# Other step durations and a minimum stay in the planner that merges TensorE's streams

## The chip, the core and the metric

One core of a Trainium2 chip runs the whole program. The time is the device time of one execution in microseconds (us); of several executions the median is given. Five engines work side by side, each through its own list of instructions in order: TensorE (PE, with its weight loads, PEld), VectorE (DVE), ScalarE (ACT), GpSimd (POOL) and SyncE (SP), which here issues the transfers.

## The reference, cut to what matters

One inference step of a decoder of two layers, for a prompt of 1024 tokens and 8 samples of one token each, all float32. Width 1024, heads of 64:

```python
def hybrid_layer(x, pos, x_prev, wkv0, kv_buf, v_first, lp):
    p = x @ w_comb                                    # q|k|v of 8 heads, r|k|v and low-rank inputs of 8 more
    q, k = rope(q, pos), rope(k, pos)
    att = dilated_attention(q, k, v)                  # three bands (128,1), (512,4), (2048,16), merged
    att = att * rsqrt(mean(att ** 2) + eps) * gain
    z = token_shift(pr, prev0, shift_mu)
    rw, v_first, S_T = rwkv7_time_mix(z, v_first, wkv0, lp)    # delta-rule state, step by step in time
    mix = concat([att, rw]) @ w_out
    x1 = layer_norm(alpha * x + mix)
    y = layer_norm(alpha * x1 + relu(x1 @ w_ff_up) ** 2 @ w_ff_down)
```

The samples do the same with a state of their own (the state update of the mixer, called decode in the kernel) and with attention over 1024 cached keys (called kv).

## The kernel before

The tokens lie along the free axis, in two halves of 512 (the second with the 8 samples behind it). Every **dense** product (in-projection, out-projection, the two products of the feed-forward part) is made of output tiles of 128 channels by 256 to 512 tokens. Operands are split into a high and a low part, so that one step over 128 inputs is three matmuls (L364, L365, L366, into a PSUM tile dps). Weights come from HBM (wr), are split by ACT (L337, wh) and DVE (L338, wl) and wait in a ring of four pieces.

Beside it run **small groups** of PE work: a few matmuls or transposes each, whose result another engine reads before the next group of the same stream can go on.

- *Stage 1* of the mixer (function stage1; groups psg, pn, pl, pt1, pt2, pbn) takes 256 tokens of a pair of heads, a unit, up to the inverses of its triangular blocks. For the second half's last unit it ends in pdv, which hands the samples' inputs to decode.
- *Stage 2* (stage2; pT1, pBV, pX, pPQ, pO, pz, pgm, pgv) is a serial chain: inverses, outputs, and from pO to pz and back the state over four blocks of 64 tokens. There are 4 pairs of 2 units in each half of each layer.
- *Attention* (attention; pS, pET, pFT, po, pof), a pair of heads at a time. Its operands are fetched by att_load (L1494: transfers stg<-d_qkv) and split by casts on ACT (L1515, L1519) and subtractions on POOL.
- *decode* (L1639 and on): from pdv through DRAM, then in four passes a load of the samples' states (ST, L1648), products on DVE and POOL and a store (L1657), then through DRAM again (d_y, then dyr, L1666) to the groups pdy, pdm and pdq.
- *post* and *kv*: projected values to time-major, and the samples' attention over their caches (pds, pdo).

What sets PE's order is the class **Streams**. Each stream is a Python generator. A step emits one group with all that follows from it on other engines, and yields what the group costs in ns, which PSUM tag it holds and for how long, and when the next group's operands will be there. Streams.run keeps a clock of its own, self.now, that only these numbers move. At each turn it goes through the streams in the order of their adding (s2, s1, att, post, kv, and dense as the last) and takes the first that is ready by its clock, else the one that will be ready first. So small groups go ahead whenever their latency, times a slack of 1.2 in the first half-layer and 2.2 later (SLK), has passed, and the dense stream fills what is left. One brake is there: where the dense stream is ready, a small stream that has done more of its phase than the dense stream has of the phase beside it (times PACE, plus LEAD; method ahead, with the table WORK of what each phase costs) is passed over. PE follows the order that comes out word for word; for the other engines the framework makes the order.

The dense stream waits for the small ones at few places, among them those where the mixer's and the attention's outputs are needed (Mix.wait: s2, at, and for the second half dec and kv): for the last half-layer this is near the end of the feed-forward part of layer 1, first half, just ahead of the groups lnc of its second LayerNorm. After it, there is nothing but dense work and LayerNorm.

```python
                if t <= self.now:                      # Streams.run, the turn's choice
                    best = (t, s)
                    break
...
                cost += 3 * (n / 2.4 + 2.5)            # dense_steps, a step's cost for n tokens
...
            yield from mixes[l, 1].wait()              # half, ahead of the last LayerNorm of layer 1, first half
```

Of the kernel before, what the change touches and what calls it, by code (L numbers as in the profile page):

```python
# [16 lines left out]
PSUM = bass.MemoryType.PSUM  # L17
# [28 lines left out]
        "dense": (519e3, 536e3, 382e3, 394e3)}  # L46
# [76 lines left out]
def _rope():  # L123
    """Cosines and signed sines of each half's positions, and of the samples' position."""
# [14 lines left out]
def bc(ap, dims):  # L139
    """View of a tile with free dims given as (stride, count) pairs."""  # L140
    return bass.AP(tensor=ap.tensor, offset=ap.offset, ap=[list(ap.ap[0])] + [list(d) for d in dims])


class Streams:
    """Merges the emission of several instruction streams so that the TensorE's program order keeps it busy.

    A stream is a generator. Each step emits one group for the TensorE (and what follows from it on the other
    engines) and yields (cost, (bank, hold), latency, next bank): the time the group takes, the PSUM tag that it
    holds and for how long, when the next group's operands are there, and the tag that the next group needs.
    A stream may also yield a function: it goes on when that returns a time."""  # L150

    def __init__(self, depth):
        self.now = 0.0
        self.depth = depth
        self.hist = {b: [] for b in depth}
        self.streams = []
        self.times = {}
        self.cost = {}
        self.phase = {}
        self.work = {}  # L160

# [15 lines left out]
    def share(self, name):  # L177
        """The part of a stream's phase that is done."""
# [3 lines left out]
    def ahead(self, s):  # L182
        """Whether a stream has done more of its phase than the last stream of the phase beside it."""
# [35 lines left out]
    def run(self):  # L219
        while self.streams:  # L220
            best = None
            main = self.ready(self.streams[-1])
            for s in self.streams:
# [3 lines left out]
                if main is not None and main <= self.now and s is not self.streams[-1] and self.ahead(s):  # L227
                    continue
# [7 lines left out]
            self.step(best[1])  # L236


def bc(ap, dims):
    """View of a tile with free dims given as (stride, count) pairs."""  # L240
# [4 lines left out]
def body(ctx, tc, I, O):  # L245
# [44 lines left out]
    def xc(t, k, c, m=1):  # L290
        """Columns of x: tile k, or the m tiles from there."""
# [20 lines left out]
    class Weights:  # L312
        """Streams weight tiles in order of use, in pieces of four K tiles split into two float32r parts."""
# [28 lines left out]
        def take(self, keep=False):  # L342
            """The next tile's pieces; those that are kept stay in the ring until release()."""
# [11 lines left out]
    def dense_steps(items, kts, xhh, xll, res):  # L355
        """Output tiles of a dense product, side by side, in steps; their PSUM tiles are appended to res."""
        pts = [bank("d", "dps") for _ in items]
        last = len(kts) - 1
        for i, (wk, kt) in enumerate(kts):
            cost = 0  # L360
            for p, (w, m, c0, n) in zip(pts, items):
# [5 lines left out]
                cost += 3 * (n / 2.4 + 2.5)  # L367
# [5 lines left out]
    def dense(items, kts, xhh, xll, evac):  # L373
        """Dense tiles with their evacuations; a generator of steps."""
        res = []
# [27 lines left out]
    def proj_specs(l, h):  # L403
        """Weight tiles of an in-projection in order of use; the first ones come once per chunk after a LayerNorm."""
# [9 lines left out]
    def rest_specs(l, h):  # L414
        wo, wu, wd = I["w_out"], I["w_ff_up"], I["w_ff_down"]

        def inx(o):
            """Where in x, while it is free, a tile's weights stay for both chunks."""
# [6 lines left out]
        def aside(o):  # L425
            """The same where the next half's operands already lie in the first tiles of x."""
# [62 lines left out]
    def state_load(l, col, n):  # L489
        """The samples' shift states as columns of x."""  # L490
# [23 lines left out]
    def shifted(l, h, mus, m, idx, put):  # L514
        """Evacuation of an in-projection tile with the token shift; put(ci, c0, n, tile) stores a chunk."""
# [25 lines left out]
    def sigmoid(e):  # L541
        """1 / (1 + e) in place, for e = exp(-x)."""
# [3 lines left out]
    def in_proj(l, h, hook=None, tail=None, then=None):  # L546
        """The in-projection of a half: the low-rank inputs, then r, k, v (shifted) and q, k, v of each pair. hook
        comes after each of the first tiles of the first chunk, tail after the first pair's r, k, v, then before the last
        q, k, v."""
# [101 lines left out]
    def rope(t, n, tabs):  # L651
        """Rotates a pair's queries or keys: the first halves of its heads in partitions 0 to 63, the second below."""
# [7 lines left out]
    def post_stream():  # L660
        """Projected values to time-major; the samples' queries, keys and values to rows."""
# [29 lines left out]
    class LayerNorm:  # L691
        """LayerNorm over the channels of src into t, chunk by chunk of the tokens; src's tiles arrive one at a
        time. The sums are taken about the mean of the first tile. If bare, t lacks the offset in the end."""
# [49 lines left out]
        def scale(self, m, behind=None):  # L743
            """The next m tiles of a chunk whose sums are there."""
# [21 lines left out]
    class Mix:  # L766
        """The out-projection's operands of a half: the mixer's rows split, the attention's rows normalised."""
# [70 lines left out]
    def half(l, h, prev=None):  # L838
        """The dense part of a layer for one half of the tokens, and the next layer's in-projection. prev is what
        the half before left to be done beside the first tiles."""  # L840
# [33 lines left out]
        def passes(tile, ln):  # L874
            """Tiles o over all chunks, chunk by chunk, with LayerNorm's sums; a chunk's end comes beside the next
            one's tiles."""
# [146 lines left out]
        elif h == 0:  # L1023
            def beside(o):
                """The half's end beside the next one's first tiles."""
# [11 lines left out]
    def init():  # L1037
        """Constants that the start doesn't need."""
# [38 lines left out]
    def stage1(l, h, p, u, s, lw, out):  # L1077
        """Everything of a unit up to the inverses of its triangular blocks."""
# [772 lines left out]
```

## Time and profile before

| | us |
|---|---|
| median of 3 runs | 3624.27 (3622.15 to 3625.78) |
| span of the profiled execution | 3630.6 |
| PE busy in it | 3287.2 (91%) |
| DVE busy | 2060.3 (57%) |
| ACT busy | 1449.6 (40%) |
| POOL busy | 972.0 (27%) |

The profiled execution took 6.3 us more than the median of the runs; a sum made on its span is brought to the runs by that. PE's busy time is made of spans that overlap: a matmul's span goes on while the next one has started, so what a matmul costs is read from the distance between starts in the timeline. [...]

### The profile page before, as it was taken

The numbers are of one execution on the slowest core, as the hardware profiler recorded it, in microseconds if no ns is written. First come the engines' busy times: TensorE is split into PE (matmuls) and PEld (weight loads), VectorE is DVE, ScalarE is ACT, GpSimd is POOL, SyncE is SP. The second block draws the span as 40 slices with busy tenths as digits, with TensorE's granted clock in tenths as the row PEclk, the third lists the DMA queues.
The fourth block names the chain that finished last, engine by engine and source line by source line (L and its number), as shares of the span: only waits on it lengthen the run. The fifth ranks groups of instructions, "written<-read, shape, count | busy, mean of one in ns | idle before, by whom it ended". The sixth has DMA issues, their size and how long they took to land.

```text
span 3630.6 us, 66265 instructions
## 1 busy us (share of the span) xinstructions
PE 3287.2 (91%) x24732; PEld 2747.8 (76%) x24732; DVE 2060.3 (57%) x4703; ACT 1449.6 (40%) x3266; POOL 972.0 (27%) x1841
## 2 busy tenths in 40 slices
PE   8797997979899998888999999798898999989998
PEld 6565776766677677677889998676675777789998
DVE  4454544665555665467655557456654564685556
ACT  4344433343343244344443335334343433453334
POOL 1323232541111322335211013334412121240012
PEclk9898998989899999998999999898898999999999
DMA  6333343524333335442333335444143333333332
GB/s 218 106 107 108 110 120 93 141 77 116 109 108 86 101 92 155 142 136 80 85 97 88 85 88 153 117 125 132 53 119 104 109 111 89 116 99 92 94 89 84
DMA packets 366249, 393.45 MB, mean 108 GB/s; under 512 B 141816, under 2 KB 218824, under 8 KB 365928
## 3 DMA queue, kind: packets, MB, share of 16 engines
q1 hardware_dynamic: 365928, 389.22, 37.4%
q8 instruction: 195, 3.19, 0.4%
q14 instruction: 126, 1.03, 0.1%
HBM read 325.16 MB, written 63.97 MB: 107 GB/s over the span
## 4 chain that ended last, share of the span: by engine, by line
PE 42%; DMA 6%; DVE 5%; ACT 2%; issue 2%; SPq 1%; POOL 1%; ACTq 0%; DVEq 0%; POOLq 0%
PE dps L364 12%; PE dps L365 11%; PE dps L366 11%; DMA stg<-d_qkv 3%; DVE t L750 1%; PE pl L1180 1%; PE pX L1274 1%; DVE wl L338 1%; PE po L1603 1%; PE pO L1350 1%; PE pS L1558 1%; DVE t L731 0%; PE pS L1546 0%; PE pO L1331 0%; PE pO L1336 0%
## 5 line engine op out<-in xcount | busy, mean ns | idle before, releaser
L364 PE MATMUL dps<-xh,wh 128*128 128x256 f32 (+3 forms) x2984 | 1015.0, 340 | 29.8 <-ACT wh L337 13.0
L365 PE MATMUL dps<-xl,wh 128*128 128x256 f32 (+3 forms) x2984 | 959.0, 321 | 8.8 <-DVE xl L753 7.0
L366 PE MATMUL dps<-xh,wl 128*128 128x256 f32 (+3 forms) x2984 | 955.2, 320 | 2.6 <-DVE wl L338 2.6
L338 DVE TENSOR_TENSOR wl<-wr,wh 128x512 fp32r<-128x512 f32 (+1 forms) x772 | 572.6, 743 | 484.1 <-ACT wh L337 462.2
L337 ACT CAST wh<-wr 128x512 fp32r<-128x512 f32 (+1 forms) x772 | 474.8, 616 | 882.9 <-PE dps L365 807.0
L364 PEld LDWEIGHTS dps<-xh,wh 128*128 128x128 f32 x2984 | 578.7, 194 | 116.1 <-issue 40.7
L365 PEld LDWEIGHTS dps<-xl,wh 128*128 128x128 f32 x2984 | 579.4, 194 | 43.1 <-DVE xl L753 10.6
L366 PEld LDWEIGHTS dps<-xh,wl 128*128 128x128 f32 x2984 | 577.7, 194 | 42.8 <-DVE wl L338 4.6
L364 PE MATMUL dps<-hh,wh 128*128 128x512 f32 (+2 forms) x1600 | 542.0, 339 | 10.6 <-DVE t L894 5.1
L365 PE MATMUL dps<-hl,wh 128*128 128x512 f32 (+2 forms) x1600 | 514.1, 321 | 3.7 <-DVE hl L936 2.3
L366 PE MATMUL dps<-hh,wl 128*128 128x512 f32 (+2 forms) x1600 | 513.4, 321 | 0.0
L364 PEld LDWEIGHTS dps<-hh,wh 128*128 128x128 f32 x1600 | 305.1, 191 | 52.8 <-issue 17.3
L366 PEld LDWEIGHTS dps<-hh,wl 128*128 128x128 f32 x1600 | 305.3, 191 | 22.5
L365 PEld LDWEIGHTS dps<-hl,wh 128*128 128x128 f32 x1600 | 305.8, 191 | 21.7 <-DVE hl L936 3.0
L1203 POOL TENSOR_TENSOR tm<-BL,XB 32x15 f32<-32x15 f32 (+7 forms) x480 | 147.1, 306 | 578.6 <-DMA BL<-d_el 521.5
L967 DVE TENSOR_TENSOR t<-dps,t 128x256 f32<-128x256 f32 (+1 forms) x240 | 123.7, 516 | 170.8 <-PE dps L366 170.1
L1205 POOL TENSOR_TENSOR XB<-XB,tm 32x15 f32<-32x15 f32 (+7 forms) x480 | 156.2, 325 | 33.8
L720 POOL TENSOR_TENSOR ln<-ln,lsq 128x256 f32<-128x256 f32 (+1 forms) x112 | 91.8, 819 | 251.2 <-ACT lsq L718 247.4
L935 DVE CAST hh<-rl 128x256 fp32r<-128x256 f32 (+2 forms) x200 | 73.5, 368 | 117.2 <-ACT rl L934 114.7
L933 ACT ACTIVATE rl<-dps 128x256 f32<-128x256 f32 (+2 forms) x200 | 88.6, 443 | 107.9 <-PE dps L366 106.2
L364 PE MATMUL dps<-hh,xh 128*128 128x256 f32 (+1 forms) x368 | 115.1, 313 | 13.1 <-DVE t L1000 6.0
L709 POOL TENSOR_TENSOR t<-t,ln 128x256 f32<-128x256 f32 (+1 forms) x32 | 28.1, 915 | 366.7 <-ACT ln L703 366.7
(346 smaller groups left out, 5192.4 us busy)
## 6 DMA issues: line engine op xcount, KB each, us to landing
wr<-in_w_ff_up SPq DMA_DIRECT2D x272, 256.0 KB
wr<-in_w_ff_down SPq DMA_DIRECT2D x256, 256.0 KB
wr<-in_w_in SPq DMA_DIRECT2D x220, 256.0 KB
stg<-d_qkv SPq DMA_DIRECT2D x128, 128.0 KB
wr<-in_w_out SPq DMA_DIRECT2D x64, 256.0 KB
z<-d_z SPq DMA_DIRECT2D x24, 384.0 KB
d_qkv<-qe SPq DMA_DIRECT2D x32, 256.0 KB
kvc<-in_cache_k SPq DMA_DIRECT2D x32, 256.0 KB
```

The source lines that it names most:

```text
L337: A.copy(h[:, :, :m], w[:, :, :m])
L338: V.tensor_tensor(lo[:, :, :m], w[:, :, :m], h.bitcast(F32)[:, :, :m], op=ALU.subtract)
L364: PE.matmul(p[:m, :n], wh[:, wk % 4, :m], hi, start=(i == 0), stop=False)
L365: PE.matmul(p[:m, :n], wh[:, wk % 4, :m], lo, start=False, stop=False)
L366: PE.matmul(p[:m, :n], wl[:, wk % 4, :m], hi, start=False, stop=(i == last))
L720: G.tensor_tensor(s2, s2, sq, op=ALU.add)
L750: V.scalar_tensor_tensor(t, t, g, self.s2[:, c], op0=ALU.mult, op1=ALU.mult)
L933: A.activation(r, p[:, :n], AF.Relu)
L935: V.tensor_copy(hh[:, c0:c0 + n], r)
L967: V.tensor_tensor(to, p[:, :n], to, op=ALU.add)
L1203: G.tensor_tensor(tv, bc(BL[:, 17 * j + 1:17 * j + 2], [(1, m), (0, j + 1)]), bc(XB[:, 16 * j:16 * j + 1], [(0, m), (1, j + 1)]), op=ALU.mult)
L1205: G.tensor_tensor(xv, xv, tv, op=ALU.add)
```

## The change

The planner's numbers and its rule of choice change; what is computed and the instructions stay.

- A dense step of n tokens costs 3 x (0.447 n + 4) ns in the planner, 699 in place of 648 for 512 tokens, and the dense phases in WORK are scaled by the same 8%.
- When the planner comes back from small groups to the dense stream, its clock moves on by SWITCH = 280 ns.
- From then on it stays with the dense stream for RUN = 3200 ns of its clock, as long as this stream is ready, whatever else is. This holds once the first half-layer's dense part has been entered ("dense" in self.phase); ahead of that there is no stay.

The docstrings of the file are emptied too.

```diff
@@ constants
 WORK = {"s2": (73e3, 74e3, 73e3, 74e3), "s1": (38e3, 42e3, 42e3, 45e3), "att": (29e3, 49e3, 29e3, 49e3),
-        "dense": (519e3, 536e3, 382e3, 394e3)}
+        "dense": (561e3, 580e3, 413e3, 427e3)}
+RUN = 3200
+SWITCH = 280
@@ Streams.__init__
         self.work = {}
+        self.stay = 0.0
+        self.away = False
@@ Streams.run
         while self.streams:
             best = None
-            main = self.ready(self.streams[-1])
+            last = self.streams[-1]
+            main = self.ready(last)
+            free = main is not None and main <= self.now
+            if free and self.now < self.stay:
+                self.step(last)
+                continue
             for s in self.streams:
                 t = self.ready(s)
                 if t is None:
                     continue
-                if main is not None and main <= self.now and s is not self.streams[-1] and self.ahead(s):
+                if free and s is not last and self.ahead(s):
                     continue
...
             self.now = max(self.now, best[0])
-            self.step(best[1])
+            if best[1] is not last:
+                at = self.now
+                self.step(best[1])
+                self.away |= self.now > at
+                continue
+            if self.away:
+                self.away = False
+                self.now += SWITCH
+                if "dense" in self.phase:
+                    self.stay = self.now + RUN
+            self.step(last)
@@ dense_steps
-                cost += 3 * (n / 2.4 + 2.5)
+                cost += 3 * (0.447 * n + 4)
```

The order of PE's instructions changes nearly everywhere behind the first groups. Two places show how.

PE, attention and stage 1 beside the feed-forward part of layer 0, first half, about a quarter into the program, before; pO0 and pz are of stage 2, pt1 and pt2 of stage 1:

```order
L1350 MATMUL pO0_10034<-FG_10006,Zp_129 64x128 x2
L364 MATMUL dps_10135<-hh_8821,wh_9925 128x512
L365 MATMUL dps_10135<-hl_8822,wh_9925 128x512
L366 MATMUL dps_10135<-hh_8821,wl_9926 128x512
L1222 MATMUL pt1_10139<-cst_79,BK_9810 128x128 x4
L364 MATMUL dps_10135<-hh_9454,wh_9925 128x512
L365 MATMUL dps_10135<-hl_9455,wh_9925 128x512
L366 MATMUL dps_10135<-hh_9454,wl_9926 128x512
L1235 MATMUL pt2_10150<-cst_79,AR_9809 128x128 x4
L1357 MATMUL pz_10156<-cst_79,St_10127 64x64 x2
```

The same groups now:

```order
L384 MATMUL dps_9708<-xh0_88,wh_9581 128x512
L385 MATMUL dps_9708<-xl0_90,wh_9581 128x512
L386 MATMUL dps_9708<-xh0_88,wl_9582 128x512
L1377 MATMUL pz_9715<-cst_79,St_9613 64x64 x2
L1242 MATMUL pt1_9720<-cst_79,BK_9415 128x128 x4
L1255 MATMUL pt2_9728<-cst_79,AR_9414 128x128 x4
```

Before, one dense step of three matmuls stood between pO0, pt1 and pt2. Now pz, pt1 and pt2 follow each other, and 15 dense matmuls stand ahead of them and 15 behind, of which three are shown.

PE, where decode ends in layer 1 (pdy, pdm, pdq; the last of the mixer's groups are pgm and pgv), before:

```order
L364 MATMUL dps<-xh_88,wh 128x512
L365 MATMUL dps<-xl_90,wh 128x512
L366 MATMUL dps<-xh_88,wl 128x512
L1387 MATMUL pgv<-gq,cst 128x256
L1674 MATMUL pdm<-a,cst 128x32
```

The same place now:

```order
L1398 MATMUL pgm<-y,cst 128x256
L1399 MATMUL pgm<-gs,gup 128x256
L1407 MATMUL pgv<-gq,cst 128x256
L1690 MATMUL pdy<-cst,dyr 128x8 x4
L1694 MATMUL pdm<-a,cst 128x32
L1699 MATMUL pdq<-a,cst 128x32
L722 MATMUL lnc<-t,onec 128x256 x2
L384 MATMUL dps<-xh_88,wh 128x512
L385 MATMUL dps<-xl_90,wh 128x512
L386 MATMUL dps<-xh_88,wl 128x512
```

Before, pdy stood six dense matmuls ahead of the first row shown and pdq eighteen behind the last, and the groups lnc come some 34 us of dense work later. Now pgm, pgv and the groups of decode follow each other without a dense matmul, and lnc, at which the dense stream waits for the small ones, comes right behind.

## Rows read from the trace of the kernel before

**Rows 1.** The page, part 1: busy us of each engine, share of the span, instructions.
```profile
PE 3287.2 (91%) x24732; PEld 2747.8 (76%) x24732; DVE 2060.3 (57%) x4703; ACT 1449.6 (40%) x3266; POOL 972.0 (27%) x1841
```

**Rows 2.** Stages: stretch, us; busy us of PE, PEld, DVE, ACT, POOL; PEclk; DMA, GB/s.
```profile
51.30:678.80 627.50, 536.64 (x4266) 430.15 (x4264) 308.19 (x845) 244.71 (x589) 205.74 (x444) 0.91 0.40 115
678.80:1359.20 680.40, 622.94 (x4368) 473.43 (x4367) 391.63 (x897) 261.80 (x591) 178.22 (x355) 0.96 0.35 98
...
1430.10:2066.30 636.20, 584.30 (x4757) 501.72 (x4756) 371.58 (x873) 260.56 (x604) 187.43 (x373) 0.95 0.36 101
...
2362.10:3073.50 711.40, 647.81 (x4754) 496.26 (x4752) 412.26 (x954) 267.29 (x618) 186.95 (x371) 0.93 0.37 106
```

**Rows 3.** PE's waits of two stages, longest row each: us, times, longest.
```profile
PE pn L1139 <- ACT sg L544: 14.7, 1, 14.7
...
PE pq L679 <- issue: 12.2, 1, 12.2
```

**Rows 4.** Timeline, 735 to 756 us: start, us, engine, line; idle before and its releaser.
```profile
745.56 0.62 ACT L1519 CAST kS<-stg 128x512 fp32r<-128x512 f32 x1 [12.03 <-DMA stg<-d_qkv]
...
753.53 1.23 PE L1139 MATMUL pn<-cst,sg 128*128 128x128 f32 x4 [14.67 <-ACT sg L544]
```

**Rows 5.** ACT's waits, whole span.
```profile
ACT kS L1519 <- DMA stg<-d_qkv: 198.9, 34, 16.6
```

**Rows 6.** Stretch behind the stall of rows 4, columns as in rows 2.
```profile
753.50:757.30 3.80, 3.77 (x24) 2.96 (x25) 3.48 (x6) 2.37 (x7) 3.44 (x5) 0.50 0.13 22
```

**Rows 7.** Timeline of PE: pz alone, pl alone, pz and pl, pbn alone.
```profile
873.13 0.39 PE L365 MATMUL dps<-hl,wh 128*128 128x512 f32 x1
873.36 0.39 PE L366 MATMUL dps<-hh,wl 128*128 128x512 f32 x1
873.68 0.33 PE L1357 MATMUL pz<-cst,St 64*64 64x64 f32 x4
...
874.28 0.40 PE L365 MATMUL dps<-hl,wh 128*128 128x512 f32 x1
...
1432.87 0.39 PE L366 MATMUL dps<-xh,wl 128*128 128x512 f32 x1
1433.19 1.71 PE L1180 MATMUL pl<-AR,BK 64*128 64x128 f32 x16
...
1435.17 0.40 PE L365 MATMUL dps<-xl,wh 128*128 128x512 f32 x1
...
861.96 0.39 PE L366 MATMUL dps<-hh,wl 128*128 128x512 f32 x1
862.28 0.33 PE L1357 MATMUL pz<-cst,St 64*64 64x64 f32 x4
862.54 1.71 PE L1180 MATMUL pl<-AR,BK 64*128 64x128 f32 x16
...
864.52 0.39 PE L365 MATMUL dps<-hl,wh 128*128 128x512 f32 x1
...
1991.65 0.28 PE L365 MATMUL dps<-hl,wh 128*128 128x256 f32 x1
1991.78 0.28 PE L366 MATMUL dps<-hh,wl 128*128 128x256 f32 x1
1991.89 0.59 PE L1239 MATMUL pbn<-sq,cst 128*128 128x256 f32 x2
...
1992.44 0.28 PE L365 MATMUL dps<-hl,wh 128*128 128x256 f32 x1
```

**Rows 8.** Timeline of PE and SP: decode's input, last transfer, first group behind.
```profile
2932.09 0.27 PE L1249 MATMUL pdv<-cst,dvt 128*40 128x128 f32 x1
...
2995.53 0.30 SPq L1666 DMA_DIRECT2D dyr<-d_y  x1
...
3030.82 0.41 PE L1670 MATMUL pdy<-cst,dyr 8*128 8x8 f32 x4
```

**Rows 9.** A stretch of the second stage with few small groups, columns as in rows 2.
```profile
998.70:1278.80 280.10, 273.32 (x1826) 204.00 (x1825) 153.27 (x319) 100.05 (x210) 61.73 (x139) 0.99 0.35 98
```

## The prediction

> **What bounds the kernel now.** I read the page first, then a table of stages, then the waits of TensorE (PE) stage by stage, then single places in the timeline. On the page [rows 1] PE is busy 91% of the span and no other engine above 57%, so the kernel is one long PE program, whose order is fixed beforehand. In it stand 14904 matmuls of the dense products and 1298 small groups of the mixer and the attention, in 764 interruptions of the dense work (counted in the order). The loss is what stands between PE's busy time and the span, 343 us, and the table of stages [rows 2] says where: 90.9 us in the first stage with small groups (51 to 679 us), and 57.5, 51.9 and 63.6 us in the three later ones (679 to 1359, 1430 to 2066, 2362 to 3074), 173 us together. The other 80 us lie in four stretches with few small groups, which the change hardly touches.
>
> Who ends these waits: PE waits rarely, 29, 21 and 25 times in the three later stages, and the longest alone takes 14.7 us in the second stage and 12.2 in the last [rows 3]; 18 of the 75 are over 3 us and hold 120 of the 173 us. What is behind the longest is seen at 738 to 754 us [rows 4]: ScalarE (ACT), which works in order, stands 12.0 us at a cast until its transfer stg<-d_qkv lands, the sigmoid behind it is late, and PE stops 14.7 us at group pn. In sum ACT waits 198.9 us at these casts [rows 5]; PE covers of a stall what dense work it has ahead of the first group that needs ACT. [...]
>
> **The change part by part.** No instruction is added or removed; the docstrings that go cost nothing. PE's order changes, and with a moved group move its evacuations on VectorE and ACT and its transfers, past the weight loads in SyncE's queue; I give that no term of its own, and the ends of the later stages' term stand for it.
>
> *Fewer interruptions.* The order has 584 instead of 764. What one costs is read where PE waits for nothing [rows 7]. From the last dense matmul to the second one behind: 0.92 us around pz alone, 2.30 around pl alone, 2.56 around pz and pl together; two dense steps (0.466) are in each, so the groups cost 0.45, 1.83 and 2.09, and joining them saves 0.19. That is the switch: pz starts 0.32 us behind the last dense matmul where dense ones follow each other at 0.23, and the dense work is late again behind it. The group pbn, which uses the whole array as the dense matmuls do, starts 0.11 behind the last one, near their own spacing of 0.13: it has no switch, and joining it to pz leaves pz's where it was. A saving comes only where two groups follow each other that both use part of the array (64 rows or columns). Such neighbours number 223 before and 260 after: 37 x 0.19 = 7 us. Taken: **-7 us**; ends 0 and -36 (all 180 at 0.2).
>
> [...]
>
> *Later stages: a minimum stay.* Behind each interruption now stand at least 3.2 us of dense work, 15 matmuls at 0.233 us or 27 at 0.12 us [rows 7]. Dense runs of at most 12 matmuls fall from 379 to 16 in all stages but the first. I took each group and its successor in the same stream (pO and pz, pS and pET, and so on) and priced the PE work between them by such rows: its median goes from 3.66, 3.61 and 3.70 us in the three later stages to 4.36, 4.13 and 4.61, its tenth percentile from 2.2 to 3.5. So a successor comes some 0.9 us later, and each wait shrinks by up to that. The 18 waits above 3 us lose 16 us; the 57 short ones (53 us, mean 0.9) lose about half, 26. Together 42 us of idle time. For the clock: 0.96, 0.95 and 0.93 in these stages [rows 2] mean half speed in 8, 10 and 14% of them, 218 us for 173 us of idle time; PE is busy in part of it and loses half of that, so I take 0.4 us more for each idle us. 42 x 1.4: **-59 us**. Ends: 0, if the stalls at stg decide alone (the casts stand as close in ACT's new order as before), and -105 (all short waits, 1.2 us of each long one, x 1.4).
>
> *First stage.* There the minimum stay isn't on yet, but dense steps cost 8% more in the planner and a return 280 ns, so small groups come earlier against the dense work: 364 instead of 333 in the same dense stretch, with 1.89 instead of 2.18 us between successors (tenth percentile 1.10 for 1.38). 25 waits longer by 0.3 us, x 1.4: **+11 us**; ends 0 and +25 (a fifth of the stage's waits).
>
> *The end of the mixer.* Because they yield to the stay, the small streams of the last stage end later: the last chain step of the mixer stood 38 us of dense work ahead of the point where the dense stream waits for the streams (the lnc groups), and now the last 26 groups ahead of pdy stand at that point with no dense matmul among them, then pdy, pdm and pdq. What decides is the samples' state update (decode): from pdv, its last input, it goes through a transfer, four passes of load, VectorE, GpSimd and store, and two more transfers before pdy can run. The rows [rows 8] show it: pdv at 2932.1, the last transfer issued at 2995.5; with some 2 us to land, 66 us. PE came to pdy at 3030.8, 99 us behind pdv, and did not wait. In the new order 54 dense matmuls (12.6 us) and 33 groups (20 us by rows like those of [rows 7]) stand between pdv and pdy, 33 us. So PE idles 33 us, in which the waits of the mixer's last unit vanish too, and its clock falls behind it: +4. **+36 us**; ends +23 (the passes run 10 us faster in all beside an idle PE) and +45.
>
> Sum: -7 - 59 + 11 + 36 = -19 us. On the profiled span of 3630.6 us that is 3611.6; the median of the runs stands 6.3 us lower, so 3605 us.
>
> **The rivals.** *The tail decides* (slower). The long stalls are ACT's, in order behind stg, and start wherever the loads stand; if dense work ahead of them only delays them, the later stages give back a third, 20 us, and the sum is -7 - 20 + 11 + 36 = +20: 3645 us; at nothing given back it is 3664. It decides as soon as the later stages give back less than 40 us with the clock, 29 of their 173 idle us. For it: 120 of the 173 us are in 18 waits, and the casts stay where they were. Against it: where small groups are thin before (999 to 1279 us, [rows 9]), PE hardly waits at all, 7 of 280 us, and the change thins them out in the other parts of these stages. *A wash:* gains of some 40 us and the tail cancel, 3617 to 3631. *More gain:* the short waits vanish, 3559. *Every interruption gives back its switch:* -36 in place of -7, 3576; for it speaks the 0.19 us of pz and pl, against it pbn. [...]
>
> **How the numbers follow.** Forecast 3605 (own range 3580 to 3616): 0.38. Tail decides: 0.30. Wash: 0.17. More gain: 0.10. Whole switches: 0.05. About 0.2%, 7 us, is what a measurement can tell here. Faster: 0.38 + 0.10 + 0.05 = 0.53; same 0.17; slower 0.30. The range from 3550 to 3660 leaves out the low end of more gain and the far end of the tail, 0.2 in all, more of it above.
>
> **What would show it.** Right: PE's busy time within 20 us of before; idle time in the later stages down by a quarter, but a stretch of some 30 us with idle PE ahead of pdy, which decode's transfer ends; more idle time before 679 us. Wrong: no wait at pdy (then decode is faster, or the streams end earlier than the order says); later stages that idle as long as before, with ACT at stg; a clock that falls without an idle stretch ahead, which the bunches of groups could bring and no stretch of before shows.

## The result: slower, and the profile after

The changed kernel takes 3672.8 us (median of 4, 3665.4 to 3676.8) for 3623.2 before: ratio 1.0136, interval 1.0121 to 1.0151, 50 us slower. I had forecast 3605, with 3550 to 3660 as the range. The sign was that of the rival "the tail decides", whose 3645 us was still 28 too low.

The page of the changed kernel, part 1, and its granted clock in 40 slices of the span; then the line of the core:

```profile
PE 3300.9 (90%) x24732; PEld 2761.1 (75%) x24732; DVE 2049.0 (56%) x4703; ACT 1445.3 (39%) x3266; POOL 975.3 (27%) x1841
PEclk9788989899999999899999999798989997999999
...
core 0: 3671.2 us, clock 0.935
```

Beside [rows 1], PE is busy 13.7 us longer with the same 24732 matmuls, the span is 40.6 us longer, and the mean clock fell from 0.944 to 0.935. The table of stages, cut at the same dense matmuls as [rows 2], with the end of the fourth stage as a stretch of its own (its last 157 dense matmuls, up to the dense step behind lnc); columns as there:

```profile
52.30:736.20 683.90, 579.64 (x4535) 459.88 (x4533) 333.20 (x890) 252.65 (x614) 221.82 (x484) 0.88 0.37 107
736.20:1383.90 647.70, 604.52 (x4099) 463.10 (x4098) 378.30 (x852) 251.77 (x564) 164.27 (x316) 0.95 0.35 101
1456.20:2071.40 615.20, 558.16 (x4530) 482.86 (x4529) 355.10 (x842) 253.65 (x589) 177.20 (x339) 0.95 0.35 103
2388.80:3007.60 618.80, 555.99 (x4119) 431.48 (x4118) 341.02 (x810) 239.52 (x555) 171.19 (x329) 0.94 0.37 108
3007.60:3111.20 103.60, 81.26 (x605) 58.89 (x603) 59.26 (x138) 26.86 (x64) 20.62 (x42) 0.81 0.33 86
```

The same end of the fourth stage in the kernel before, full and at the high clock:

```profile
3035.90:3073.50 37.60, 37.59 (x165) 30.29 (x163) 19.44 (x38) 12.99 (x23) 0.00 (x0) 1.00 0.35 95
```

Lengths alone mislead, because small groups moved from one stage to another. So I split each stage of both traces into three: PE idle; **clock loss**, which is half of PE's busy time while the granted clock (PEclk, a share of full speed) was at 0.50 (counted as if the work would have taken half as long; the clock's records in both traces hold 0.50 and 1.00 alone, with 49 falls to 0.50 before and 52 after, so a PEclk between them holds both); and the rest, work at the full clock. Half is a little too much: dense matmuls of 512 tokens follow each other every 0.427 us where the granted clock is 0.50 and every 0.233 us where it is 1.00. That moves no change in the table by more than 3 us.

| us | before | after | change | forecast |
|---|---|---|---|---|
| first stage, idle | 90.9 | 104.3 | +13 | |
| first stage, clock loss | 36.5 | 59.8 | +23 | first stage in all +11 |
| second to fourth, idle | 173.0 | 163.0 | -10 | -42 |
| second to fourth, clock loss | 77.0 | 64.6 | -12 | -17 |
| ahead of lnc, idle + clock loss | 0 | 32.6 | +33 | +36 |
| elsewhere, idle + clock loss | 99.0 | 107.0 | +8 | 0 |
| work at full clock | 3154.2 | 3139.8 | -14 | -7 |

The sum is the 40.6 us of the two spans. The other 9 of the 50 us stand in no row: the profiled span of before lies 7.4 us above the median of its runs, that of the changed kernel 1.6 us below. The end of the mixer cost what it was said to cost, the switches gave a little more, 8 us elsewhere had been put at nothing, and two terms were wrong: the first stage by 26 us, the later stages by 37.

**The end of the mixer** is seen in the timeline of the changed kernel, PE and SP, from just before the last dense matmul ahead of lnc up to lnc (start, us, engine, line; idle before):

```profile
3045.74 0.35 SPq L1272 DMA_DIRECT2D d_dec<-dT  x1
...
3066.77 0.51 PE L1294 MATMUL pT<-X,LB 64*64 64x64 f32 x10 [0.56 <-ACT gq L1408]
...
3075.82 0.48 PE L1294 MATMUL pT<-X,LB 64*64 64x64 f32 x4 [5.29 <-DVE XT L1326]
...
3105.63 0.30 SPq L1686 DMA_DIRECT2D dyr<-d_y  x1
...
3105.85 1.22 PE L1407 MATMUL pgv<-gq,cst 128*128 128x256 f32 x2 [1.31 <-ACT gq L1404]
3107.20 0.59 PE L1690 MATMUL pdy<-cst,dyr 8*128 8x8 f32 x4
...
3109.70 2.05 PE L722 MATMUL lnc<-t,onec 128*128 128x256 f32 x4
```

No dense matmul stands between 3061.7 and 3111.2 us. Decode's last transfer is issued 61 us behind pdv (3045.0; 63 in [rows 8]). But there is no single wait of 33 us at pdy: the mixer's last unit, a serial chain now without dense work to cover it, fills the same 50 us with 18 waits over 0.15 us (22.2 us) and with work at a granted clock of 0.50 (a loss of 10.3), and pgv ends just as dyr lands, for which pdy's weight load waits 0.8 us. Both chains end together, so the price was right and its place only half.

### The profile page after: what moved, and what is told of

The parts are those of the page before. It is cut to its first block, busy times and chain, and to the rows that moved or that the text cites. A ratio compares the mean times of both kernels' runs of the same rounds, so it can differ in the third digit from the quotient of the medians.

```text
span 3671.2 us, 66184 instructions
## 1 busy us (share of the span) xinstructions
PE 3300.9 (90%) x24732; PEld 2761.1 (75%) x24732; DVE 2049.0 (56%) x4703; ACT 1445.3 (39%) x3266; POOL 975.3 (27%) x1841
## 5 line engine op out<-in xcount | busy, mean ns | idle before, releaser
L384 PEld LDWEIGHTS dps<-xh,wh 128*128 128x128 f32 x2984 | 584.2, 196 | 121.9 <-issue 36.8
L384 PE MATMUL dps<-hh,wh 128*128 128x512 f32 (+2 forms) x1600 | 531.0, 332 | 16.4 <-DVE t L985 9.6
L1586 ACT ACTIVATE E<-E,mx 128x384 f32<-128x384 f32 (+4 forms) x128 | 80.1, 626 | 98.0 <-DVE mx L1585 97.5
```

Of the source, the lines that this page charges most:

```text
L384: PE.matmul(p[:m, :n], wh[:, wk % 4, :m], hi, start=(i == 0), stop=False)
L1586: A.activation(E[:, :f + w], E[:, :f + w], AF.Exp, bias=mx[:, 4 + hd:5 + hd], scale=0.125, accum_out=mx[:, 6 + hd:7 + hd])
```

## The experiments

All are edits of the kernel before or of the changed one; "prices" are the planner's two numbers, the new dense durations (with WORK) and the 280 ns per return to dense work. Times in the text are medians, ratios are to runs of the kernel before on the same chip. The theories behind the expectations: **A**, the prices crowd the first stage and the stay leaves work over ahead of lnc; **B**, the stay and its bunches cost by themselves; **C**, the stretch ahead of lnc is nearly all of it; **D**, formed on the way, any other order costs, wherever its waits happen to fall.

### Stay and prices apart

`no_stay`: the changed kernel with `RUN = 0`.

> The changed kernel with the minimum stay at nothing (RUN = 0): the new dense durations and the 280 ns per return to dense work are left. By the accounts of the two traces (first stage +37 us with its clock, the exposed stretch ahead of lnc +33, less elsewhere) theory A says that the prices alone crowd the first stage: in the order 1588 small matmuls stand there against 1413 before and 1552 in the changed kernel, so the first stage should lose 30 to 45 us against before as the changed kernel does, no stretch without dense work ahead of lnc, and the time 3645 to 3665 us. The rival B says that the stay and its bunches cost all of it: then this is before's time within 0.3%, 3613 to 3634 us, and its first stage lies within 10 us of before's 627.

`stay_only`: the old durations and WORK, `SWITCH = 0`, `RUN = 3200`.

> The kernel before (its dense durations, no price for a return) with the minimum stay of 3200 ns alone. Theory A: the first stage is that of before (1408 small matmuls in it against 1413), so within 10 us of 627; the later stages gain some 20 us in idle time and clock and some 10 in switches; ahead of lnc more small work is left than in the changed kernel (324 matmuls of the small groups against 239), so 35 to 50 us are lost there; 3625 to 3650 us. Rival B: the stay costs by itself, 3660 us and more.

Measured: no_stay 3676.2 us (1.0145, 1.0122 to 1.0169), stay_only 3663.1 (1.0108, 1.0089 to 1.0126). Both lie above theory A's ranges; stay_only stands where B put it, no_stay does not. Each part costs by itself, and the two costs don't add up. The tables of stages, first stage of no_stay, then first stage, fourth stage and the stretch up to lnc of stay_only:

```profile
51.40:741.40 690.00, 584.22 (x4597) 463.35 (x4595) 336.59 (x900) 256.38 (x626) 226.41 (x498) 0.88 0.37 108
```
```profile
52.70:676.90 624.20, 538.45 (x4261) 432.43 (x4259) 309.62 (x837) 243.53 (x586) 210.59 (x452) 0.90 0.39 115
2359.90:2972.90 613.00, 551.55 (x4048) 429.50 (x4047) 340.72 (x795) 232.15 (x530) 164.67 (x330) 0.94 0.38 110
2972.90:3105.80 132.90, 96.05 (x759) 69.30 (x757) 69.24 (x175) 38.30 (x94) 23.66 (x47) 0.78 0.25 66
```

The first stage goes with the prices: 690 us and clock 0.88 with them, 624 and 0.90 without. What the stay costs sits ahead of lnc: 36.8 us idle and 12.3 of clock in 133 us.

### The stretch ahead of lnc

`stay_not_last` (on the changed kernel) and `stay_only_not_last` (on stay_only) switch the stay off in the fourth stage:

```diff
-                if "dense" in self.phase:
+                if "dense" in self.phase and self.phase["dense"][0] < 2:
                     self.stay = self.now + RUN
```

> The changed kernel, but the minimum stay is off in the last of the four stages with small groups (dense phase 2 and on); up to there the order is the changed kernel's, and behind it the streams end before lnc as they did before. Theory A: the 33 us of the exposed stretch go, the fourth stage loses its share of the gain (10 to 15 us): 3640 to 3660 us, with the first stage at 684. A theory C, that the exposed stretch is nearly all of the loss: 3622 to 3636 us.

> The kernel before with the minimum stay of 3200 ns alone, off in the last of the four stages. If the 49 us lost ahead of lnc with the stay alone are lost for good, they go, the fourth stage returns to some 99 us of idle time and clock (86 with the stay), and the time is 3620 to 3635 us, 30 to 40 below the stay alone. If that stretch only holds time that is otherwise lost in the fourth stage, the time stays at 3650 to 3665 us.

Measured: stay_not_last 3674.8 us (1.0137, 1.0114 to 1.0161), as slow as the changed kernel and above both ranges, since its fourth stage lost 29 us more (112.4 for 83.0) while the 33 ahead of lnc went, and its first stage, in the same order, 10 more; so far apart can two profiled executions of one order lie. stay_only_not_last 3631.6 (1.0017, 1.0006 to 1.0029), 31 below stay_only and within the range for time lost for good. Its fourth stage and the stretch up to lnc:

```profile
2362.80:3028.90 666.10, 597.14 (x4616) 453.43 (x4615) 382.79 (x928) 254.47 (x595) 189.76 (x377) 0.95 0.38 108
3028.90:3070.30 41.40, 41.40 (x190) 32.44 (x188) 21.40 (x46) 14.73 (x29) 0.00 (x0) 1.00 0.35 91
```

The stretch is full again, at clock 1.00, and the fourth stage holds 87.9 us of idle time and clock loss, 86.0 with the stay: without the prices the 49 us were lost time, not moved time, and 31 of them came back in the medians. With the prices in, the fourth stage takes 29 of the 33 back and the time stays, so there undoing this stretch gained nothing.

### Which price

`switch_only` and `durations_only`: the kernel before with one price alone. `durations_switch140`: the durations with 140 ns. `durations_stay3200`: the changed kernel with `SWITCH = 0`, so one part undone.

> The kernel before with one part alone: 280 ns on the planner's clock at each return to dense work; the old dense durations, no stay. Its order has 1562 small matmuls in the first stage (1413 before, 1552 changed, 1588 with the durations too). Theory A (the first stage's loss follows from how much small work is planned into it): first stage longer by 33 to 45 us in idle time and clock, nothing ahead of lnc; 3655 to 3675 us. Rival D (any re-ordering costs about 1.2%, since the kernel before is the best of many orders, and the place of the loss has nothing to do with the amount of small work): about the same time, but with the loss spread over the stages, less than 20 us of it in the first.

> The kernel before with the new dense durations and work alone (some 8% more per dense step in the planner), no price for a return, no stay. 1457 small matmuls in the first stage (1413 before, 1552 changed), 787 interruptions. Theory A (loss follows the amount of small work planned into the first stage): a third of the first stage's loss, 3630 to 3642 us. Theory D (any other order than that of before costs, by how its waits happen to fall): 3640 to 3675 us with the loss in no fixed stage. If the durations alone carry the changed kernel's first stage (the 280 ns alone left that stage at 644 us), its length is 675 us or more.

> The new durations with half the price of a return (140 ns), no stay. 1534 small matmuls in the first stage (1457 with the durations alone, 1588 with 280 ns). Theory A, graded: the first stage's loss of idle time and clock lies between 120 us (durations alone) and 164 (both), at 140 to 155, and the time at 3630 to 3655 us. Theory D, by how the waits fall in each order: anything from 3600 to 3675, the first stage either near 120 to 130 or near 165.

> The changed kernel without the 280 ns per return to dense work: new durations and the minimum stay of 3200 ns. If the first stage's loss needs both prices, that stage is at 620 to 640 us; 334 small matmuls are left ahead of and at lnc (324 with the stay alone, 239 in the changed kernel), so some 45 us are lost there, and the time is 3630 to 3655 us. If the prices have nothing to do with it and the stay's later stages do, it stays at 3665 to 3680 us.

| | us, median | ratio, interval | first stage, idle + clock loss |
|---|---|---|---|
| switch_only | 3650.8 | 1.0069 (1.0046 to 1.0093) | 120 |
| durations_only | 3601.7 | 0.9936 (0.9919 to 0.9953) | 120 |
| durations_switch140 | 3671.6 | 1.0126 (1.0106 to 1.0147) | 152 |
| no_stay (280 ns) | 3676.2 | 1.0145 | 164 |
| durations_stay3200 | 3614.8 | 0.9974 (0.9962 to 0.9985) | 116 |
| after (280 ns) | 3672.8 | 1.0136 | 164 |

The profiled execution of switch_only took 3632 us and its four others 3650 to 3655, so its 120 tells little. Of the other times, durations_only lies below both its ranges, durations_switch140 above theory A's (its first stage is in A's 140 to 155) and durations_stay3200 below its own. Without the 280 ns the changed kernel is 0.26% **faster** than before, a difference within the scatter shown below, although it still loses 43 us ahead of lnc. First stage and the stretch up to lnc of durations_stay3200, then the first stage of durations_only and of durations_switch140:

```profile
51.60:673.10 621.50, 537.00 (x4320) 431.74 (x4319) 316.68 (x851) 245.10 (x591) 221.78 (x469) 0.91 0.40 116
...
2926.40:3050.90 124.50, 95.24 (x747) 68.65 (x746) 68.03 (x163) 35.10 (x86) 22.75 (x46) 0.79 0.29 77
```
```profile
51.70:680.00 628.30, 540.87 (x4342) 433.93 (x4341) 319.39 (x860) 246.67 (x597) 224.22 (x469) 0.91 0.40 116
```
```profile
52.20:722.20 670.00, 559.45 (x4497) 445.65 (x4495) 332.01 (x881) 251.52 (x617) 218.60 (x470) 0.90 0.38 110
```

The four kernels with the new durations and 280 ns (no_stay, after, stay_1600, stay_not_last) hold 164 to 174 us in the first stage; the four with the new durations, no return price and the casts left on ACT (durations_only, durations_stay3200 and the two of the last section) hold 116 to 123. The return price costs in each of three pairs: 0.7% on the old durations, which is no more than neighbouring orders differ by (below), 2.1% on the new ones, 1.6% with the stay. The durations gained 0.6% alone and 1.3% beside the stay, and cost 0.8% beside the return price.

### Half the stay, and the durations the other way

`stay_1600`: the changed kernel with `RUN = 1600`. `stay_alone_1600`: the same stay without the prices. `dense_cheaper`: `n / 2.6` for `n / 2.4` and WORK times 0.92 in the kernel before.

> The changed kernel with half the minimum stay (1600 ns): its order has 660 interruptions (764 before, 584 with 3200 ns) and no stretch without dense work ahead of lnc. Theory A: first stage as in the changed kernel (+37), no exposed stretch, later stages with half the gain: 3640 to 3655 us. Theory C, the exposed stretch is nearly all of the loss: 3620 to 3632 us. Rival B, bunches cost by themselves: half of the changed kernel's loss, 3645 us too, but then with the first stage at some 655 and the loss in the later ones.

> The kernel before with a minimum stay of 1600 ns alone: 681 interruptions (764 before), first stage as before (1413 small matmuls), and no stretch without dense work ahead of lnc. Theory A: the first stage within 10 us of 627, 5 us less switching, some 5 to 10 us gained in the later stages: 3605 to 3622 us. Rival D (any re-ordering costs): 3650 us and more.

> The opposite sign: the kernel before with its dense steps made some 8% shorter in the planner (n / 2.6 for n / 2.4, and the work of the dense stream times 0.92), no price for a return, no stay. The order has 1383 small matmuls in the first stage (1413 before) and as many interruptions as before (765). Theory A: the first stage loses 5 to 10 us less than before, the rest as before: 3608 to 3624 us. Rival D (any re-ordering costs): 3645 us and more, with a first stage that is no better.

Measured: stay_1600 3673.1 us (1.0136, 1.0115 to 1.0157), above all its ranges, first stage again 690 us long at clock 0.87; stay_alone_1600 3613.9 (0.9976, 0.9965 to 0.9987), within theory A's range; dense_cheaper 3650.3 (1.0079, 1.0058 to 1.0101), where theory A failed and D's figure came true: with less small work in the first stage (1383 matmuls for 1413) it lost 11 us more there and 10 more in the fourth.

### How far apart are neighbouring orders?

`nudge_up` and `nudge_down`: each dense step 3 ns longer or shorter in the planner, under half a per cent.

> The kernel before with each dense step 3 ns longer in the planner (3 * (n / 2.4 + 3.5) for + 2.5, under half a per cent): a change that means nothing, but moves groups by a dense step here and there; 782 interruptions (764 before), 1435 small matmuls in the first stage (1413). Theory D: slower than before by 0.4% to 1.3%, 3638 to 3670 us, though nothing of substance is changed. Theory A: within 0.3% of before, 3613 to 3634 us.

> The same with each dense step 3 ns shorter in the planner (+ 1.5 for + 2.5): 775 interruptions, the first stage's order nearly as before (1413 small matmuls). Theory D: slower than before by 0.4% to 1.3% in the stages whose order moves (the second to the fourth), first stage within 8 us of 627. Theory A: within 0.3% of before.

Measured: nudge_up 3640.8 us (1.0040, 1.0025 to 1.0055), nudge_down 3610.6 (0.9962, 0.9950 to 0.9974), both outside theory A's 0.3% and only the first where D put it. A change that means nothing moves this kernel by 0.4% either way, 14 and 16 us. The traces tell little of where: nudge_up's profiled execution idles 20 us more than that of the kernel before, but loses 18 us less to the clock, and is 4 us longer; nudge_down idles 18 us less and loses 12 less. So neither "any other order is slower" nor "only the amount of small work counts" holds, and what a single order gains or loses below some 0.5% says nothing of the rule that made it. Two nudges are no bound either: the 0.8% of dense_cheaper has no account.

### ScalarE's waits at stg

The rival rested on ACT's waits at the casts behind stg<-d_qkv, 198.9 us by [rows 5]. That row is only the keys' cast; with the queries' the kernel before waits 330 us there, the changed one 351 (193.7 and 157.4). The row of before that is missing:

```profile
ACT qS L1515 <- DMA stg<-d_qkv: 131.5, 20, 15.8
```

`before_castpool` moves both casts to POOL (`A.copy` becomes `G.tensor_copy`), TensorE's order stays; `best` and `durations_castpool` do it to stay_alone_1600 and to durations_only.

> The kernel before, with the two casts that wait for the transfers stg<-d_qkv moved from ScalarE to GpSimd, which waits for the same transfers anyway; TensorE's order stays. If ScalarE's 330 us of waits at these casts stand behind much of TensorE's long waits (the reason given for the rival in which the stay gives little), idle time of the four stages falls by 40 to 100 of their 264 us and the time by 40 to 130 us, less what the longer casts cost on GpSimd. If those waits only happen to stand beside TensorE's, the time is within 15 us of before, or slower, because GpSimd's own groups stand behind the casts.

> The kernel before with the two things that gained: the minimum stay of 1600 ns alone (0.24% measured) and the two casts behind stg<-d_qkv on GpSimd (0.59%). If the gains add up, 3592 us, 0.8% below before; if the stay gained by the same waits that the casts cause, about 3600 us.

> The kernel before with the new dense durations alone (0.64% faster as measured) and the two casts behind stg<-d_qkv on GpSimd (0.59%). Two gains that add up give 3580 us; if the times of orders only scatter around a mean near before's, and the good order of the durations rested on its waits as they were, 3595 to 3625 us.

Measured: before_castpool 3602.4 us (0.9941, 0.9926 to 0.9956), best 3607.3 (0.9950, 0.9935 to 0.9966), durations_castpool 3640.8 (1.0049, 1.0034 to 1.0064). The first, 21 us faster, lies between its two cases; the other two lie above theirs. Waits of before_castpool, ACT's longest, then POOL's at the casts (us, times, longest):

```profile
ACT wh L337 <- PE dps L365: 865.4, 528, 13.2
ACT E L1566 <- DVE mx L1565: 126.1, 57, 10.5
...
POOL kS L1519 <- DMA stg<-d_qkv: 188.1, 31, 14.8
...
POOL qS L1515 <- DMA stg<-d_qkv: 130.0, 20, 15.4
```

ACT no longer waits there at all, yet PE's idle time rose by 5 us (348.2 for 343.3), because its waits moved to other engines. The keys' cast takes as long on POOL, 0.61 us for 0.62 in the median, not longer as I had assumed, so it is not the casts' length. As the profile puts it, PE's waits that ACT ends fell from 156 to 58 us; those that POOL ends rose from 14 to 99, and those that transfers end from 13 to 59. PE's waits for the group of [rows 4], before:

```profile
PE pn L1139 <- ACT sg L544: 30.2, 5, 14.7
```

With the casts on POOL, the longest and that group:

```profile
PE pT L1274 <- DMA X<-d_el: 40.6, 12, 12.1
PE lnq L734 <- POOL ln L720: 36.9, 3, 16.7
PE pS L1557 <- POOL kS L1520: 33.2, 3, 20.3
...
PE pn L1139 <- ACT sg L544: 10.0, 4, 6.6
```

So ACT's standing at the casts was behind much of PE's idle time, but POOL, where the casts now stand, makes PE wait as long; what a kernel without this standing on any engine would take stays open. What fell is the clock loss, 99 for 133 us, with 38 falls of the clock for 49. On the order of durations_only the same edit cost 1.1%, 28 us of it in the first stage, whose order it does not touch: timing on the other engines moves the time as widely as the order does.

### The parts that gained, put together

`durations_stay_not_last`: durations_stay3200 with the stay off in the fourth stage. `durations_stay1600`: durations and half the stay.

> The changed kernel without the return price (new durations, stay of 3200 ns), with the stay off in the last of the four stages, so that nothing is left ahead of lnc (the order has 20 matmuls of small groups from there to the end, as before, for 193 and more with the stay). By the account of the durations with the stay throughout: 43 us lost ahead of lnc go, the fourth stage takes 8 to 20 back, its switches some 6: 3580 to 3600 us, 0.7 to 1.2% faster than before. If the scatter between orders decides (as the two nudged kernels show, some 0.4% either way), 3600 to 3630.

> The changed kernel without the return price and with half the stay (1600 ns): 666 interruptions, first stage as with the durations alone (1453 small matmuls for 1457), nothing left ahead of lnc. By the accounts: the durations alone gave 3602, the stay of 1600 ns alone 10 us less than before, so 3590 to 3602 us. If the scatter between orders decides: 3602 to 3630.

Measured: 3615.0 us (0.9942, 0.9928 to 0.9955) and 3616.5 (0.9943, 0.9931 to 0.9955); on that chip the kernel before took 3635.4. Both lie above what the account gave and where the scatter would put them. The first gained 0.3% on durations_stay3200, for 17 to 29 us (0.5 to 0.8%) by the account: the 43 us went, and the fourth stage took 25 back (109.1 for 83.7). Of all kernels here four lie at 0.6% below before, and none lower. Of the eleven times that theory A forecast one came true (stay_alone_1600); it told the place of a loss better than its size.

## Why the prediction was wrong, step by step

**Fewer interruptions: right, -14 for -7.** Work at full clock fell in all three pairs with and without the stay of 3200 ns: by 11.9 us for 178 interruptions fewer (stay_only), 16.3 for 200 (durations_stay3200 against durations_only), 18.2 for 205 (after against no_stay). That is 0.07 to 0.09 us for an interruption that goes. The rival by which each gives back 0.2 us is out. That two groups on part of the array save 0.19 us where they follow each other is read at pz and pl [rows 7]; no run measured it by itself.

**Later stages, -22 us for -59: here the prediction failed.** Forecast were 42 us of idle time less; it became 10, and the clock gave 12 for 17. Here is PE's idle time in the second to fourth stage, parted by who waits, a small group or the dense stream itself (dense matmuls and the groups of the normalisations):

| us | small groups wait | dense stream waits |
|---|---|---|
| before, stay_only | 138, 117 | 35, 65 |
| durations_only, durations_stay3200 | 141, 93 | 22, 51 |
| no_stay, after | 160, 111 | 21, 52 |

From before to after the waits at small groups fell by 27 us, for the 42 forecast, and those of the dense stream rose by 17. In the pairs with and without the stay, it takes 21, 48 and 49 us off the waits at small groups and gives 29 to 31 back at the dense stream. The step that failed is the choice to count only the successors of small groups, and to let all their waits shrink alike: those that ACT ends, by the profile, went from 73 to 69 us, all others from 65 to 42. So far the rival "the tail decides" was right, and its 20 us for these stages came near the 22 measured; what it missed is the first stage. The parting scatters too: at the dense stream nudge_up, without a stay, has 51 us, and before_castpool, in the order of before, 58. So it is the three pairs that speak for the new wait, and no single kernel. Waits of the dense stream in the second stage, longest rows of the kernel before (us, times, longest):

```profile
PE dps L364 <- DVE t L1000: 2.6, 2, 1.8
...
PE dps L364 <- DVE hh L935: 2.4, 1, 2.4
...
PE dps L365 <- DVE xl L753: 1.8, 4, 0.8
```

The same of the changed kernel:

```profile
PE dps L384 <- ACT wh L357: 5.3, 1, 5.3
PE dps L384 <- ACT xh L772: 4.7, 3, 3.3
...
PE dps L384 <- DVE t L987: 2.9, 1, 2.9
...
PE lnq L754 <- POOL ln L740: 2.6, 1, 2.6
...
PE dps L384 <- DVE hh L955: 2.4, 1, 2.4
...
PE dps L385 <- DVE xl L773: 1.6, 4, 0.7
```

They are the dense stream's own operands: the split weights, the split activations, the evacuated tiles. Before, dense work idled 11 us in this stage, now 26. That an interruption used to give ACT and DVE the time to get these ready is argued from the rows; no run measured it by itself. My other guess, that short waits shrink by half, fell with it: waits of up to 3 us were 52.7 us in the three stages and are 61.7, while those above 3 us went from 120.3 to 101.2, near the 16 us forecast.

**First stage, +37 for +11, the second term that failed; the clock is the larger part.** The idle time was sized about right (+13 for 8). The clock was not: I took 0.4 us of clock for each us of idle time, from the later stages, and here 13 us of idle came with 23 of clock. Instead of 12 falls of the clock there are 15, and PE is busy in 119.7 of their 163.8 us for 73.0 of 112.6. Three stretches at the low clock in the first stage of the changed kernel, columns as in [rows 2]:

```profile
173.00:183.20 10.20, 9.66 (x81) 7.39 (x76) 7.09 (x11) 3.91 (x11) 2.83 (x2) 0.50 0.41 138
193.40:213.90 20.50, 16.95 (x90) 12.57 (x90) 8.14 (x20) 4.73 (x10) 2.78 (x3) 0.50 0.35 102
548.40:558.60 10.20, 10.20 (x65) 6.66 (x62) 5.33 (x24) 2.18 (x7) 0.00 (x0) 0.50 0.13 40
```

PE is busy nearly throughout and half of that is loss by this account; 78 of 81, 84 of 90 and 54 of 65 matmuls are of small groups. The first begins behind a wait of only 3.40 us at pT. That the return price is behind it was shown by undoing it: durations_stay3200 holds 116 us there for 164. Its 280 ns move the planner's clock without any dense work done, so a small group comes due earlier in the real order. That it costs in this stage because the slack is 1.2 here and not 2.2 is argued; no run changed the slack. On the old durations the 280 ns alone left 120 us there in its one profiled execution, so it takes both prices, as far as that trace tells. With both, the median distance between a group and its successor, counted in the order as in the prediction, is 1.89 us of PE work, 2.18 before and 2.27 with the durations alone. I had seen the 1.89 and laid it to the change as a whole. Why 1.89 costs 37 us, while the 2.10 of durations_switch140 costs 25 and the 2.27 of durations_castpool 20, the runs leave open: distance is not the only thing that counts.

**The end of the mixer: right in size**, 33 us (36 forecast, though its 33 and 4 make 37), seen again in stay_only (49, with more groups left) and in the pair with stay_only_not_last (31 us by the medians). No run shows the 4 us of clock as such: behind the stall of [rows 4] PE ran 3.8 us at 0.50 [rows 6], a loss of 1.9 by the account above, and in this stretch 22.3 us of idle time came with 10.3 of clock loss. As a price of its own it does not hold in the changed kernel, where stay_not_last took it away and gained nothing.

**What I left out: the scatter.** No term stood for what a changed order does merely by being another. Two nudges that mean nothing gave +0.4% and -0.4%, so the own range of 3580 to 3616 was too narrow, and the sign could not rest on a sum of -19 us. The parts do not come back one by one: the return price undone gave 58 us (3672.8 to 3614.8), more than the first stage's 37, and the stay off in the fourth stage gave nothing. What is shown is that the return price turns this change from a small gain into a loss; how the 50 us fall on single waits lies partly within the scatter.

## What to carry to other kernels

When an order is changed, part the bound engine's idle time by who waits: keeping one stream on the engine longer moved waits from the others to it in three pairs. A price on a planner's clock that no engine work answers to makes everything else come due early; and a stream that yields must still end before the point where all are awaited. Before reading meaning into half a per cent of a re-ordered kernel, measure what a meaningless nudge of its order does, and put that into the range.

## What the runs showed of the hardware

Over the twenty traces here, what PE loses to a granted clock of 0.50 goes with how often the clock fell to it, 38 to 55 times (correlation 0.89), and little with the sum of PE's idle time (0.36). before_castpool idles 5 us more than the kernel before, in fewer pieces (125 waits over 0.15 us for 140); its clock falls 38 times for 49, and it loses 34 us less. Behind a wait of 3.40 us the changed kernel's PE ran 10.2 us at a granted clock of 0.50, busy for 9.66 of them.
